# Block 2 of a two-block trunk: weights of four leading tiles split ahead of the stage before, norm sums on TensorE alone, transposed-weight dots in block 1 only

## The chip, the cores and the metric

One NeuronCore of a Trainium2 chip. The metric is the device time of one execution in microseconds, the median of several runs. The kernel before took 1892.75 us (three runs, 1886.89 to 1897.9).

## The reference

Two transformer trunks follow one another on 256 tokens of width 1024. The first (block 1) has two layers with modulation, pooled, gated and latent attention mixers, and an MLP; its first layer also carries 256 context tokens. The second (block 2) has two layers, and each of them is

```
mod = silu(c) @ w_ada[l] + b_ada[l]            # six vectors of 1024
h = rmsnorm(x, g_mix_pre) * (1 + scale_a) + shift_a
y = hybrid_mixer(h, w_in, ...) @ w_out         # three attentions
x = x + gate_a * rmsnorm(y, g_mix_post)
h = rmsnorm(x, g_ffn_pre) * (1 + scale_f) + shift_f
x = x + gate_f * rmsnorm((silu(h @ w_g) * (h @ w_u)) @ w_down, g_ffn_post)
```

with a hidden width of 2816. Everything is float32.

## The kernel before

**Products.** A float32 product is made of three products of rounded parts: high by high, high by low, low by high (lines 150 to 152, the helper `mm` at L131). Activations stand transposed, 128 features on the partitions, 256 tokens along the row. A weight piece is brought from HBM by SP's queue (`wraw`, 1 MB, two buffers), and `split` turns each half of it, a granule of 128 x 1024, into `whi` (a cast on ScalarE, L134) and `wlo` (a subtraction on VectorE, L135), with two buffers of each. A granule serves 24 matmuls. So a piece can be loaded two ahead and split one or two ahead of TensorE.

**Order.** The kernel is written as a recording in program order; a scheduler then fixes one list per engine, and each engine runs its list in order and waits by semaphores. What stands in a list ahead of a waiting instruction is done, what stands behind it is not.

**Hand-overs of block 2.** Between two big stages stands a chain: the last product gives `y`, the squares of `y` (`Post`) give `st`, from that come `ms` (VectorE), its power -0.5 (POOL), and a transposed copy `bc`; then for each of eight chunks k `update(k)` forms `post = y * G * bc` and `x = x + post`, and `Lead.chunk(k)` forms `xa = x * A` in a high part (ScalarE) and a low part (VectorE). TensorE doesn't wait for the next rmsnorm: it multiplies the unnormed `xa` by the first four tiles of the next weight matrix, chunk by chunk (`lead`), into the banks pa and pS, then two more tiles into pg and pmod (`tiles_x`). The norm's scale `rr` comes meanwhile (`norm_stats`) and is multiplied in when the tiles are read out (`lead_out`, which forms `lb`, `sgl`, `swu`). The following tiles get their granules by the common rings, and `h` is formed only then.

The function `first` (from L1035) does this for the weights w: `early` splits two tiles of w[0] into the rings, `early_act` splits two tiles of w[1] into eight small tiles `wact`, `early_more` two tiles of w[2] into `wmore0` and `wmore1`. All three are called at the start of `first`, so after the products of the stage before. w is w_in_2a of layer 0, w_gate_up of layer 0, w_in_2a of layer 1, and w_gate_up of layer 1. The stage ahead of a w_gate_up is w_out_2, whose input `mixc` has eight chunks: four are multiplied while the last mixers still run, the other four here, in four pieces (`gemm_half`; 24 products each, `x<-pa,x` at L1080 adds the parts).

**Sums of squares.** `norm_stats` squares the eight chunks on ScalarE (`sq`, L1109), POOL adds the first six (L1113), and TensorE sums over partitions by one-column products with ones (`pqt`): three pairs, one for the sum and two for the last chunks. In `update` the additions `x = x + post` (L1479) are on VectorE for k in ADDV = 1, 3, 5, 7 and on POOL for the others.

**Dots.** Part of the modulation vectors are products of a transposed weight row block with silu(c): 512 KB brought by SP (`wdot`, three buffers) and one VectorE instruction with a running sum (L436) for each 128 values; 128 such dots in all. They are queued as due, and every weight piece gives a credit of `self.pace`; a whole credit runs one dot. The pace is 3.25 in the MLP of block 1's layer 0, 0.75 in layer 1, 0.75 in the feed-forward of block 2 while any are due.

Of the kernel before, what the change touches and what calls it, by code (L numbers as in the profile page):

```python
# [21 lines left out]
S = 256  # L22
DFF = 2816
EPS = 1e-6
ADDV = 1, 3, 5, 7
PACE1 = 3.4
GAN = 1152
RAWN = 2080
# [2 lines left out]
class K:  # L31
# [994 lines left out]
    def block2(self):  # L1026
        tc, nc, a = self.tc, self.nc, self.a
        y = [x[:, 256:512] for x in self.x]
        with ExitStack() as es:
            act = es.enter_context(tc.tile_pool(name="bact", bufs=16, reuse_waits="tile"))  # L1030
            self.pump()
            self.pace = 0
            xs = [x[:, :256] for x in self.x]

            def first(stage, w, mods, f=None):  # L1035


                self.early(w[0], 2, 8)
                self.early_act(w[1], act)
                xp = stage.enter_context(tc.tile_pool(name="xin2", bufs=1, reuse_waits="tile"))  # L1040
                with tc.tile_pool(name="wmore", bufs=1, side="right", reuse_waits="tile") as wmp:
                    more = self.early_more(w[2], wmp)
                    lead = Lead(self, xp, mods)
                    if f:
                        f.rstd()
                    for k in range(8):
                        if f:
                            f.update(k)
                        lead.chunk(k)
                    o = self.lead(lead.xa, 4, by_k=f is not None)  # L1050
                    rr = xp.tile([128, 512], F32, name="rr")
                    out = self.norm_stats(rr[:, :256]) if f else self.first_stats(rr)
                    o = [p[0] for p in o]
                    for p in self.tiles_x(lead.xa[0], more=more, banks=(self.psum("pg"), self.pm.tile([128, 512], F32, name="pmod", tag="pmod"))):
                        o.append(p)
                        if len(o) == 5:
                            out()
# [9 lines left out]
            stage = ExitStack()  # L1067
            for l in range(2):
                m = lambda s: self.mod(1, l, s)[:, 0]
                if l == 0:  # L1070
                    A = self.gain(self.g_pre[:, l], m(1), "A10")
                    nc.vector.tensor_mul(A, A, self.g_final)
                    o = first(stage, a["w_in_2a"][0], [(0, 256, A, m(0))])
                with tc.tile_pool(name=f"bmix{l}", bufs=1, reuse_waits="tile") as mp:
                    mix = self.mixers2(l, *o, act, mp, y)
                    self.act_set("silu_and_others")
                    f = Post(self, y)

                    def ev(k, o):
                        nc.vector.tensor_add(y[k], o, y[k])  # L1080
                        f.chunk(k)
                    for i in range(4):
                        self.gemm_half(a["w_out_2"][l, i], mix, 0, 0, 256, lambda j, o, i=i: ev(2 * i + j, o))
                    del mix
                stage.close()
                f.gain(self.g_post[:, l], m(2))
                o = first(stage, a["w_gate_up"][l], [(0, 256, self.gain(self.f_pre[:, l], m(4), "A20"), m(3))], f)
                if self.due:
                    self.dots_begin(stage.enter_context(tc.tile_pool(name="dw2", bufs=1, reuse_waits="tile")))
                    self.pace = 0.75  # L1090
                with tc.tile_pool(name=f"bhid{l}", bufs=16, reuse_waits="tile") as hp:
                    f = self.ffn(l, *o, hp, y, act)
                self.dots_end()
                self.pace = 0
                stage.close()
                if l == 0:
                    f.gain(self.f_post[:, l], m(5))
# [343 lines left out]
class Post:  # L1441
# [193 lines left out]
```

## Time and profile before

| quantity | value |
|---|---|
| median of three runs | 1892.75 us |
| profiled execution | 1901.53 us, span 1899.8 us |
| mean granted clock of TensorE in it | 0.949 of full speed |
| TensorE busy | 1735.2 us (91%), 11998 matmuls |
| VectorE busy | 1243.1 us (65%) |
| ScalarE busy | 848.9 us (45%) |
| POOL busy | 242.9 us (13%) |
| HBM read | 297.72 MB, 157 GB/s over the span |

All durations below are of the profiled execution. Block 1 ends near 1160 us. The w_out_2 products of layer 0 end near 1311 us, its feed-forward near 1520 us, the w_out_2 products of layer 1 near 1677 us, its feed-forward near 1889 us. The granted clock is a share of 2.4 GHz; a stretch at 0.62 is a mixture of the two levels 2.4 and 1.2 GHz. Where a matmul's own time is shown, neighbours overlap in it; the distance from start to start tells what one costs.

### The profile page before, as it was taken

Reading aid. Unit: us, or ns where it says so; the run is one execution under the profiler, and the core shown is the slowest. Engines: PE = TensorE matmul, PEld = TensorE weight load, DVE = VectorE, ACT = ScalarE, POOL = GpSimd, SP = SyncE. Lnnn points to the kernel's source line nnn. Section 1 sums busy time; section 2 is a strip of 40 time slices with the busy share of each in tenths; the row PEclk is TensorE's granted clock in tenths of the full one; section 3 lists DMA queues with packets and bytes.
Section 4 is the critical chain, followed back from the end, with each engine's and each line's share of the span. In section 5 each row is a group of like instructions: output and inputs, shape, how many; then the busy total and the mean of one; then the engine's idle time right before and its main releaser. Section 6 shows DMA issues by size and latency. Waiting matters only on the chain.

```text
span 1899.8 us, 30418 instructions
## 1 busy us (share of the span) xinstructions
PE 1735.2 (91%) x11998; PEld 1484.0 (78%) x11998; DVE 1243.1 (65%) x2401; ACT 848.9 (45%) x1626; POOL 242.9 (13%) x264
## 2 busy tenths in 40 slices
PE   5998899989999999888989999797899989988997
PEld 3766546868777888874778999687899978788997
DVE  3237776588988846557778666657854665575555
ACT  3243434353222234544454446555444455554443
POOL 2025310110000001243110001202100031021000
PEclk9998989989999999997989999898999988989998
DMA  8533231287877622311278554216455523143553
GB/s 328 200 111 123 83 107 30 93 285 286 283 279 283 212 90 91 116 51 38 64 266 296 181 181 159 97 38 233 167 178 184 185 99 107 47 143 133 178 181 131
DMA packets 66639, 300.75 MB, mean 158 GB/s; under 512 B 9472, under 2 KB 13492, under 8 KB 45760
## 3 DMA queue, kind: packets, MB, share of 16 engines
q1 hardware_dynamic: 65744, 297.74, 45.0%
q8 instruction: 95, 1.56, 0.3%
q0 software_dynamic: 464, 1.05, 0.2%
q14 instruction: 48, 0.39, 0.1%
q10 hardware_dynamic: 288, 0.01, 0.0%
HBM read 297.72 MB, written 1.05 MB: 157 GB/s over the span
## 4 chain that ended last, share of the span: by engine, by line
PE 67%; DVE 12%; DMA 6%; ACT 3%; POOL 3%; issue 2%; ACTq 0%; SPq 0%; POOLq 0%; DVEq 0%
PE pa L131 48%; PE pS L131 6%; PE pb L131 3%; PE pg L131 3%; DVE wlo L135 3%; PE pO L131 3%; DMA wdot<-in_w_ada_t_dram 2%; DVE wdot L436 2%; DMA wdot<-in_w_mod_t_dram 1%; PE pmod L131 1%; PE pPT L942 1%; ACT whi L134 1%; DMA mraw<-in_w_mod_dram 1%; DVE Qz L815 1%; DVE nt L354 1%
## 5 line engine op out<-in xcount | busy, mean ns | idle before, releaser
L134 ACT CAST whi<-wraw 128x1024 fp32r<-128x1024 f32 (+4 forms) x398 | 371.1, 934 | 577.7 <-PE pa L131 519.8
L135 DVE TENSOR_TENSOR wlo<-wraw,whi 128x1024 fp32r<-128x1024 f32 (+4 forms) x398 | 434.5, 1094 | 232.0 <-ACT whi L134 231.2
L131 PE MATMUL pa<-h,whi 128*128 128x256 f32 (+1 forms) x2400 | 532.7, 318 | 9.9 <-ACT h L358 6.0
L131 PEld LDWEIGHTS pa<-h,whi 128*128 128x128 f32 x2400 | 399.0, 193 | 44.6 <-ACT h L358 7.4
L131 PE MATMUL pa<-h,wlo 128*128 128x256 f32 (+1 forms) x1200 | 381.5, 318 | 2.3 <-DVE wlo L135 2.1
L131 PE MATMUL pa<-hid,whi 128*128 128x256 f32 (+1 forms) x1728 | 378.0, 315 | 0.2
L131 PEld LDWEIGHTS pa<-hid,whi 128*128 128x128 f32 x1728 | 282.7, 188 | 23.6 <-issue 1.8
L131 PE MATMUL pa<-hid,wlo 128*128 128x256 f32 (+1 forms) x864 | 273.3, 316 | 8.7 <-DVE wlo L135 8.5
L131 PEld LDWEIGHTS pa<-h,wlo 128*128 128x128 f32 x1200 | 231.1, 193 | 20.6 <-DVE wlo L135 4.0
L131 PEld LDWEIGHTS pa<-hid,wlo 128*128 128x128 f32 x864 | 162.6, 188 | 22.7 <-DVE wlo L135 11.8
L436 DVE SCALAR_TENSOR_TENSOR wdot<-wdot,cb 128x1024 f32<-128x1024 f32 x128 | 155.9, 1228 | 25.2 <-DMA wdot<-in_w_ada_t_dram 14.5
L131 PE MATMUL pa<-mixc,whi 128*128 128x256 f32 (+1 forms) x512 | 121.5, 325 | 4.0 <-ACT whi L134 1.0
L131 PEld LDWEIGHTS pa<-mixc,whi 128*128 128x128 f32 x512 | 85.9, 194 | 16.9 <-issue 2.7
L131 PE MATMUL pa<-xa,whi 128*128 128x258 f32 x448 | 92.4, 300 | 6.4 <-ACT whi L134 4.5
L131 PE MATMUL pb<-whi,h 128*128 128x256 f32 (+2 forms) x448 | 93.4, 300 | 3.5 <-ACT h L358 3.3
L499 DVE SCALAR_TENSOR_TENSOR x<-pa,mod,x 128x256 f32<-128x256 f32 x144 | 63.0, 479 | 40.9 <-PE pa L131 40.3
L131 PEld LDWEIGHTS pb<-whi,h 128*128 128x128 f32 x448 | 74.1, 197 | 10.9 <-issue 6.1
L131 PE MATMUL pa<-mixc,wlo 128*128 128x256 f32 (+1 forms) x256 | 81.4, 320 | 1.0 <-DVE wlo L135 1.0
L131 PEld LDWEIGHTS pa<-xa,whi 128*128 128x128 f32 x448 | 76.5, 206 | 7.0 <-ACT whi L134 4.9
L329 POOL TENSOR_TENSOR sq<-sq 128x512 f32<-128x512 f32 (+1 forms) x15 | 18.9, 1260 | 427.8 <-ACT sq L325 427.8
L131 PE MATMUL pa<-xa,wlo 128*128 128x258 f32 x224 | 66.4, 299 | 3.5 <-DVE wlo L135 3.5
L131 PE MATMUL pb<-wlo,h 128*128 128x256 f32 (+2 forms) x224 | 65.9, 297 | 0.9 <-DVE wlo L135 0.9
(383 smaller groups left out, 2525.8 us busy)
## 6 DMA issues: line engine op xcount, KB each, us to landing
wdot<-in_w_ada_t_dram SPq DMA_DIRECT2D x96, 512.0 KB, 5.6
wraw<-in_w_gate_up_dram SPq DMA_DIRECT2D x44, 1024.0 KB, 4.9
wraw<-in_w_up_dram SPq DMA_DIRECT2D x32, 1024.0 KB, 4.9
wraw<-in_w_down_dram SPq DMA_DIRECT2D x32, 1024.0 KB, 5.7
mraw<-in_w_mod_dram SPq DMA_DIRECT2D x48, 512.0 KB, 4.2
wdot<-in_w_mod_t_dram SPq DMA_DIRECT2D x32, 512.0 KB, 5.4
wraw<-in_w_down_2a_dram SPq DMA_DIRECT2D x16, 1024.0 KB, 4.9
wraw<-in_w_in_2a_dram SPq DMA_DIRECT2D x12, 1024.0 KB, 4.8
```

The lines of the kernel that those rows point to most:

```text
L131: self.last = self.nc.tensor.matmul(out, l, r, start=start, stop=stop, **k).ins
L134: self.nc.scalar.copy(hi, src)
L135: self.nc.vector.tensor_sub(lo, src, hi)
L329: (eng or nc.vector).tensor_add(s, s, q)
L354: nc.vector.scalar_tensor_tensor(t[:, s], self.x[k][:, s], A[:, k:k + 1], bc[:, s], op0=ALU.mult, op1=ALU.mult)
L436: nc.vector.scalar_tensor_tensor(w, w, 1.0, c, op0=ALU.mult, op1=ALU.mult, accum_out=o[:, j:j + 1])
L499: nc.vector.scalar_tensor_tensor(self.x[n][:, s], o[:, s], gate()[:, r, n:n + 1], self.x[n][:, s], op0=ALU.mult, op1=ALU.add)
L815: nc.vector.tensor_mul(z[rows, :, r], e[rows], q[rows])
L942: nc.tensor.transpose(pt[:, n * 128:(n + 1) * 128], P[:, 0, n * 128:(n + 1) * 128], self.ident)
```

## The change

1. A new function `prepare(w)` opens the memory of the next hand-over and does the splits of w[1] (`wact`) and w[2] (`wmore`). It is called ahead of the w_out_2 products (both layers) and ahead of the last quarter of the down products (`down(2)` of layer 0). `first` then only splits w[0] and goes on. The raw piece of `wmore` gets a buffer of its own (`wmraw`).
2. `norm_stats` makes no POOL additions: all eight squares go to TensorE, 16 one-column products in place of 6, from one ring of two buffers.
3. `update` makes all its eight additions on VectorE (ADDV is gone).
4. The pace of the dots is 3.6 and 1.15 in block 1; block 2 runs none.

```diff
     def early_more(self, src, pool):
-        raw = self.raw_piece(src, 2048)
+        raw = pool.tile([128, 2048], F32, name="wmraw")
+        self.nc.sync.dma_start(raw, src)
...
-                self.pace = (3.25, 0.75)[l]
+                self.pace = (3.6, 1.15)[l]
...
+            def prepare(w):
+                stage.close()
+                xp = stage.enter_context(tc.tile_pool(name="xin2", bufs=1, side="right", reuse_waits="tile"))
+                wmp = ExitStack()
+                wm = wmp.enter_context(tc.tile_pool(name="wmore", bufs=1, side="right", reuse_waits="tile"))
+                self.early_act(w[1], act)
+                return w, xp, wmp, self.early_more(w[2], wm)
-            def first(stage, w, mods, f=None):
+            def first(prep, mods, f=None):
+                w, xp, wmp, more = prep
                 self.early(w[0], 2, 8)
-                self.early_act(w[1], act)
-                xp = stage.enter_context(tc.tile_pool(name="xin2", bufs=1, reuse_waits="tile"))
-                with tc.tile_pool(name="wmore", bufs=1, side="right", reuse_waits="tile") as wmp:
-                    more = self.early_more(w[2], wmp)
-                    lead = Lead(self, xp, mods)
+                lead = Lead(self, xp, mods)
...
-                    self.act_set("silu_and_others")
-                    f = Post(self, y)
+                self.act_set("silu_and_others")
+                prep = prepare(a["w_gate_up"][l])
+                f = Post(self, y)
...
-                o = first(stage, a["w_gate_up"][l], [(0, 256, self.gain(self.f_pre[:, l], m(4), "A20"), m(3))], f)
-                if self.due:
-                    self.dots_begin(stage.enter_context(tc.tile_pool(name="dw2", bufs=1, reuse_waits="tile")))
-                    self.pace = 0.75
+                o = first(prep, [(0, 256, self.gain(self.f_pre[:, l], m(4), "A20"), m(3))], f)
...
     def norm_stats(self, rr):
-        s = None
         for k in range(8):
-            q = self.tp.tile([128, 512], F32, name="sq", tag="sq" if k else "ssq", bufs=2)[:, :256]
+            q = self.tp.tile([128, 512], F32, name="sq", tag="sq", bufs=2)[:, :256]
             nc.scalar.activation(q, xs[k], AF.Square)
-            if k == 0:
-                s = q
-            elif k < 6:
-                nc.gpsimd.tensor_add(s, s, q)
-            if k >= 5:
-                for i in range(2):
-                    self.mm(st[:, i:i + 1], (s if k == 5 else q)[:, i * 128:(i + 1) * 128], self.ones[:, :1], k == 5 and i == 0, k == 7, skip_group_check=True)
+            for i in range(2):
+                self.mm(st[:, i:i + 1], q[:, i * 128:(i + 1) * 128], self.ones[:, :1], k == 0 and i == 0, k == 7, skip_group_check=True)
...
         if l == 0:
+            prep = prepare(a["w_in_2a"][1])
             f = Post(self, y)
         down(2)
...
-        (nc.vector if k in ADDV else nc.gpsimd).tensor_add(x, x, t)
+        nc.vector.tensor_add(x, x, t)
```

How the lists change is shown at three places of layer 1's hand-over (w_out_2 to w_gate_up). First ScalarE, from the last `mixc` (before). `whi_16468` belongs to w_out's third piece (the pieces 0 and 1, the latter `whi_16428`, stand ahead of it), `sq` are the squares of `y`.

```order
L134 CAST whi_16428<-wraw_16426 128x1024
L1403 ACTIVATE gsq_16234,gss_16235<-on_16173 128x256
L1414 ACTIVATE mixc_15199<-pot_16242,c_g_group_8211 128x128
L1414 ACTIVATE mixc_15200<-pot_16242,c_g_group_8211 128x128
L134 CAST whi_16468<-wraw_16466 128x1024
L1452 ACTIVATE sq_16407<-x_85 128x256
L1452 ACTIVATE sq_16423<-x_85 128x256
```

The same place now, where `whi_16434` is piece 0, `whi_16473` piece 1, `whi_16513` piece 2:

```order
L133 CAST whi_16434<-wraw_16432 128x1024
L1412 ACTIVATE mixc_15202<-pot_16245,c_g_group_8248 128x128
L1412 ACTIVATE mixc_15203<-pot_16245,c_g_group_8248 128x128
L1450 ACTIVATE sq_16452<-x_85 128x256
L133 CAST wmore0_16425<-wmraw_16423 128x1024
L133 CAST wmore1_16428<-wmraw_16423 128x1024
L1450 ACTIVATE sq_16468<-x_85 128x256
L133 CAST whi_16473<-wraw_16471 128x1024
L133 CAST whi_16513<-wraw_16511 128x1024
```

Ahead of the last `mixc` only piece 0 is split, and the casts of `wmore` and one square more stand ahead of piece 1. On VectorE the list from the same `mixc` was this, with `wlo_16429` of piece 1 four rows earlier:

```order
L135 TENSOR_TENSOR wlo_16429<-wraw_16426,whi_16428 128x1024
L295 TENSOR_SCALAR ms_16238<-gss_16235 128x1
L1406 TENSOR_SCALAR on_16173<-on_16173,grs_16237 128x256
L1415 SCALAR_TENSOR_TENSOR mixc_15199<-pot_16242,c_g_group_8211,mixc_15199 128x128
L1415 SCALAR_TENSOR_TENSOR mixc_15200<-pot_16242,c_g_group_8211,mixc_15200 128x128
L1080 TENSOR_TENSOR x_85<-pa_16393,x_85 128x256
L1080 TENSOR_TENSOR x_85<-pa_16409,x_85 128x256
L135 TENSOR_TENSOR wlo_16469<-wraw_16466,whi_16468 128x1024
```

And now it is this, with `wlo_16435` of piece 0 and `wlo_16474` of piece 1:

```order
L134 TENSOR_TENSOR wact_16414<-wraw_16397,wact_16414 128x256
L134 TENSOR_TENSOR wlo_16435<-wraw_16432,whi_16434 128x1024
L1413 SCALAR_TENSOR_TENSOR mixc_15202<-pot_16245,c_g_group_8248,mixc_15202 128x128
L1413 SCALAR_TENSOR_TENSOR mixc_15203<-pot_16245,c_g_group_8248,mixc_15203 128x128
L1089 TENSOR_TENSOR x_85<-pa_16438,x_85 128x256
L1089 TENSOR_TENSOR x_85<-pa_16454,x_85 128x256
L134 TENSOR_TENSOR wmore0_16425<-wmraw_16423,wmore0_16425 128x1024
L134 TENSOR_TENSOR wmore1_16428<-wmraw_16423,wmore1_16428 128x1024
L1454 TENSOR_TENSOR sq_16452<-sq_16452,sq_16468 128x256
L134 TENSOR_TENSOR wlo_16474<-wraw_16471,whi_16473 128x1024
```

The two `wmore` subtractions, which stood among the `xa` of the lead, and the eight `wact`, which stood ahead of `ms`, are here. On TensorE the end of the lead was followed by the three pairs of one-column products (`pqt`), by `pg`, and by the copy of the norm's scale (`c_ident,rs`):

```order
L131 MATMUL pa_16661<-xa0_16606,wlo_16563 128x258
L131 MATMUL pqt_16759<-ones_92,sq_16761 128x1 x2
L131 MATMUL pqt_16759<-ones_92,sq_16780 128x1 x2
L131 MATMUL pqt_16759<-ones_92,sq_16784 128x1 x2
L131 MATMUL pg_16791<-xa0_16606,wmore0_16600 128x258 x20
L1122 MATMUL pqt_16817<-c_ident_90,rs_16760 128x128 x2
```

Now there are eight pairs, the last four of them as follows:

```order
L130 MATMUL pqt_16762<-ones_92,sq_16780 128x1 x2
L130 MATMUL pg_16799<-xa0_16609,wmore0_16425 128x258 x2
L130 MATMUL pqt_16762<-ones_92,sq_16784 128x1 x2
L130 MATMUL pg_16799<-xa0_16609,wmore0_16425 128x258 x8
L130 MATMUL pmod_16800<-xa0_16609,wmore1_16428 128x258 x2
L130 MATMUL pqt_16762<-ones_92,sq_16788 128x1 x2
L130 MATMUL pmod_16800<-xa0_16609,wmore1_16428 128x258 x3
L130 MATMUL pqt_16762<-ones_92,sq_16792 128x1 x2
L130 MATMUL pmod_16800<-xa0_16609,wmore1_16428 128x258 x6
L1119 MATMUL pqt_16825<-c_ident_90,rs_16763 128x128 x2
```

The copy of the scale stands behind 31 of the `pg` and `pmod` products, where it stood behind 20. The lists also hold 105 dots in layer 0 of block 1 and 23 in layer 1, and none in block 2.

## Rows read from the trace of the kernel before

**Rows 1.** The page's chain that ended last, share of the span by engine.

```profile
PE 67%; DVE 12%; DMA 6%; ACT 3%; POOL 3%; issue 2%; ACTq 0%; SPq 0%; POOLq 0%; DVEq 0%
```

**Rows 2.** Stretches at T3: us from:to, length, busy (x) by engine, PEclk, DMA.

```profile
1662.00:1676.00 14.00, 13.14 (x92) 12.32 (x92) 8.84 (x18) 6.51 (x13) 0.00 (x0) 0.90 0.55 186
1676.00:1689.50 13.50, 6.38 (x31) 5.69 (x31) 11.14 (x22) 8.29 (x19) 4.95 (x6) 0.62 0.42 156
...
1709.00:1733.00 24.00, 17.69 (x119) 16.70 (x117) 14.57 (x28) 11.85 (x22) 5.00 (x4) 0.86 0.26 88
```

**Rows 3.** Stretches from the first post of T1 and T3 to the feed-forward's end.

```profile
1314.00:1520.30 206.30, 197.96 (x1608) 196.31 (x1608) 134.66 (x212) 95.96 (x154) 13.47 (x14) 0.97 0.54 185
1682.50:1889.00 206.50, 197.90 (x1607) 196.63 (x1607) 121.13 (x182) 95.69 (x153) 15.38 (x14) 0.97 0.45 153
```

**Rows 4.** Dots alone in two stretches; sum of all engines, 440 to 682 us.

```profile
400.00:690.00 290.00, 110.84 (x182) 1.00 0.72 257
...
1303.00:1358.00 55.00, 12.16 (x20) 0.88 0.61 214
...
sum 242.00, PE 235.89 PEld 188.51 DVE 204.46 ACT 70.51 POOL 0.00; mean PE 47.18 PEld 37.70 DVE 40.89 ACT 14.10 POOL 0.00
```

**Rows 5.** Lines by form, from 1150 us: xcount | busy us, mean ns | idle before.

```profile
L135 DVE TENSOR_TENSOR wlo<-wraw,whi 128x1024 fp32r<-128x1024 f32 x150 | 183.8, 1227 | 112.0 <-ACT whi L134 111.7
...
L134 ACT CAST whi<-wraw 128x1024 fp32r<-128x1024 f32 x150 | 156.8, 1047 | 193.1 <-PE pa L131 188.6 <-DMA wraw<-in_w_gate_up_dram 1.8 <-DMA wraw<-in_w_in_2a_dram 1.3
...
L1113 POOL TENSOR_TENSOR sq<-sq 128x256 f32<-128x256 f32 x15 | 13.1, 871 | 9.9 <-ACT sq L1109 5.6 <-issue 3.7
...
L1479 POOL TENSOR_TENSOR x<-x,post 128x256 f32<-128x256 f32 x12 | 11.3, 942 | 8.7 <-DVE post L1478 8.5
```

**Rows 6.** Timeline of VectorE at T3: start us, length us, instruction [idle before].

```profile
1664.89 0.76 DVE L1080 TENSOR_TENSOR x<-pa,x 128x256 f32<-128x256 f32 x2 [1.42 <-PE pa L131]
...
1678.08 2.77 DVE L135 TENSOR_TENSOR wact<-wraw,wact 128x256 fp32r<-128x256 f32 x8
1680.76 0.15 DVE L295 TENSOR_SCALAR ms<-st 128x2 f32<-128x2 f32 x1
1682.48 1.27 DVE L1478 SCALAR_TENSOR_TENSOR post<-x,pg,bc 128x256 f32<-128x256 f32 x3 [1.57 <-PE bc L1468]
...
1685.65 2.89 DVE L135 TENSOR_TENSOR wmore<-wraw,wmore 128x1024 fp32r<-128x1024 f32 x2
1688.46 1.83 DVE L1438 SCALAR_TENSOR_TENSOR xa<-x,A,xa 128x256 fp32r<-128x256 f32 x2
...
1690.55 0.47 DVE L1438 SCALAR_TENSOR_TENSOR xa<-x,A,xa 128x256 fp32r<-128x256 f32 x1
```

**Rows 7.** Timeline of ScalarE at T3, the first squares of y.

```profile
1666.05 0.72 ACT L1452 ACTIVATE sq<-x 128x256 f32<-128x256 f32 x2
```

**Rows 8.** Timeline of TensorE at T3.

```profile
1664.02 0.63 PE L131 MATMUL pa<-mixc,whi 128*128 128x256 f32 x2
...
1665.37 0.51 PE L131 MATMUL pa<-mixc,whi 128*128 128x256 f32 x2 [0.24 <-DVE x L1080]
...
1666.19 0.40 PE L131 MATMUL pa<-mixc,whi 128*128 128x256 f32 x2
...
1684.36 0.80 PE L131 MATMUL pS<-xa,wact 128*128 128x258 f32 x2 [1.92 <-ACT xa L1437]
...
1699.23 1.40 PE L131 MATMUL pqt<-ones,sq 128*128 128x1 f32 x12
...
1715.43 0.50 PE L131 MATMUL pa<-xa,whi 128*128 128x258 f32 x2 [3.74 <-ACT whi L134]
```

**Rows 9.** Timeline of VectorE at T3, after the lead.

```profile
1700.67 0.16 DVE L295 TENSOR_SCALAR ms<-pqt 128x2 f32<-128x2 f32 x1 [1.01 <-PE pqt L131]
...
1703.79 0.42 DVE L209 TENSOR_TENSOR sgl<-pa,rr 128x256 f32<-128x256 f32 x1 [0.46 <-ACT rr L1123]
```

**Rows 10.** Timeline of VectorE at T2.

```profile
1522.63 2.76 DVE L135 TENSOR_TENSOR wact<-wraw,wact 128x256 fp32r<-128x256 f32 x8
```

More of the change, by code (lines that the diff above doesn't have):

```diff
@@ L24 @@
 EPS = 1e-6
-ADDV = 1, 3, 5, 7
 PACE1 = 3.4
@@ L1033, in block2 @@
             xs = [x[:, :256] for x in self.x]
-            def first(stage, w, mods, f=None):
-                self.early(w[0], 2, 8)
-                self.early_act(w[1], act)
-                xp = stage.enter_context(tc.tile_pool(name="xin2", bufs=1, reuse_waits="tile"))
-                with tc.tile_pool(name="wmore", bufs=1, side="right", reuse_waits="tile") as wmp:
-                    more = self.early_more(w[2], wmp)
-                    lead = Lead(self, xp, mods)
-                    if f:
[L1045 to L1057, printed above, removed]
@@ new lines, in block2 @@
+            stage = ExitStack()
+            def prepare(w):
[7 more added lines that the diff above has]
+                w, xp, wmp, more = prep
+                self.early(w[0], 2, 8)
+                lead = Lead(self, xp, mods)
+                if f:
+                    f.rstd()
+                for k in range(8):
+                    if f:
+                        f.update(k)
+                    lead.chunk(k)
+                o = self.lead(lead.xa, 4, by_k=f is not None)
+                rr = xp.tile([128, 256 if f else 512], F32, name="rr")
+                out = self.norm_stats(rr[:, :256]) if f else self.first_stats(rr)
+                o = [p[0] for p in o]
+                for p in self.tiles_x(lead.xa[0], more=more, banks=(self.psum("pg"), self.pm.tile([128, 512], F32, name="pmod", tag="pmod"))):
+                    o.append(p)
+                    if len(o) == 5:
+                        out()
+                wmp.close()
@@ L1065, in first @@
                 return o, lead.xa[0], rr[:, :256], rest
-            stage = ExitStack()
             for l in range(2):
@@ L1072, in block2 @@
                     nc.vector.tensor_mul(A, A, self.g_final)
-                    o = first(stage, a["w_in_2a"][0], [(0, 256, A, m(0))])
+                    o = first(prepare(a["w_in_2a"][0]), [(0, 256, A, m(0))])
                 with tc.tile_pool(name=f"bmix{l}", bufs=1, reuse_waits="tile") as mp:
                     mix = self.mixers2(l, *o, act, mp, y)
-                    self.act_set("silu_and_others")
-                    f = Post(self, y)
-                    def ev(k, o):
-                        nc.vector.tensor_add(y[k], o, y[k])
-                        f.chunk(k)
@@ L1082, in block2, with ev @@
[L1082 to L1085, printed above, removed]
+                self.act_set("silu_and_others")
+                prep = prepare(a["w_gate_up"][l])
+                f = Post(self, y)
+                def ev(k, o):
+                    nc.vector.tensor_add(y[k], o, y[k])
+                    f.chunk(k)
+                for i in range(4):
+                    self.gemm_half(a["w_out_2"][l, i], mix, 0, 0, 256, lambda j, o, i=i: ev(2 * i + j, o))
@@ L1086, in block2 @@
+                del mix
                 f.gain(self.g_post[:, l], m(2))
-                o = first(stage, a["w_gate_up"][l], [(0, 256, self.gain(self.f_pre[:, l], m(4), "A20"), m(3))], f)
-                if self.due:
-                    self.dots_begin(stage.enter_context(tc.tile_pool(name="dw2", bufs=1, reuse_waits="tile")))
-                    self.pace = 0.75
+                o = first(prep, [(0, 256, self.gain(self.f_pre[:, l], m(4), "A20"), m(3))], f)
                 with tc.tile_pool(name=f"bhid{l}", bufs=16, reuse_waits="tile") as hp:
-                    f = self.ffn(l, *o, hp, y, act)
@@ L1093, in block2 @@
-                self.dots_end()
-                self.pace = 0
-                stage.close()
+                    f, prep = self.ffn(l, *o, hp, y, act, prepare)
                 if l == 0:
                     f.gain(self.f_post[:, l], m(5))
-                    o = first(stage, a["w_in_2a"][1], [(0, 256, self.gain(self.g_pre[:, 1], self.mod(1, 1, 1)[:, 0], "A10"), self.mod(1, 1, 0)[:, 0])], f)
+                    o = first(prep, [(0, 256, self.gain(self.g_pre[:, 1], self.mod(1, 1, 1)[:, 0], "A10"), self.mod(1, 1, 0)[:, 0])], f)
@@ L1099, in block2 @@
                 else:
                     self.post(y, self.f_post[:, l], m(5))
+            stage.close()
     def norm_stats(self, rr):
@@ L1168, in post, with ffn @@
             (nc.vector if k % 2 else nc.gpsimd).tensor_add(self.x[k][:, :256], self.x[k][:, :256], t)
-    def ffn(self, l, lead, xa, rr, rest, hp, y, act):
+    def ffn(self, l, lead, xa, rr, rest, hp, y, act, prepare):
         nc, a = self.nc, self.a
         self.ep = hp
-        f, h = None, []
+        f, prep, h = None, None, []
         groups = [range(0, 8), range(8, 16), range(16, 22)]
@@ L1234, in ffn @@
         if l == 0:
+            prep = prepare(a["w_in_2a"][1])
             f = Post(self, y)
         down(2)
-        return f
+        return f, prep
     def mixers2(self, l, lead, xa, rr, rest, act, mp, y):
```

## The prediction

> **What bounds the kernel now.** The chain of waits comes first: two thirds of the span end on TensorE [rows 1], so an edit pays or costs only where TensorE waits, or where its clock is low. The table by stretches shows where that is in the last layer: TensorE is nearly full while the second half of w_out is multiplied, then busy for 6.38 of 13.5 us at a granted clock of 0.62, and for 17.69 of 24 us further on [rows 2]. The same three stretches recur at each hand-over of block 2. I call them T1 (w_out to gate_up, layer 0), T2 (down to w_in, layer 1), T3 (w_out to gate_up, layer 1), and T0 for the entry from block 1. T3 is worked out in full, since the others carry the same instructions. In the timeline of T3 the reader follows three engines that each run their list in order: VectorE subtracts weights, then forms `ms`, waits for `bc`, runs `post` [rows 6]; ScalarE casts and squares [rows 7]; TensorE waits for either [rows 8].
>
> **1. The pace of the dots.** Block 2 loses its 11 dots, all in T1's feed-forward stage (x20 in the row counts each dot's read of the accumulator as well) [rows 4]. They were 11 times 1.23 us of VectorE, 13.5 us, but from the same point of T1 and of T3 the stages last 206.30 and 206.50 us, with 134.66 and 121.13 us of VectorE [rows 3]: with the dots and without them TensorE needs the same. Their removal is worth 0, by these two rows. The 11 go into layer 0 of block 1 (105 there instead of about 94). From 440 to 682 us of that stage TensorE is idle for 242.00 - 235.89 = 6.1 us while 110.84 us of dots and their reads run in the somewhat longer stage [rows 4]. If that idle time is the dots' own, a dot costs below 0.1 us, and 11 cost +1. The ends are 0 (all slack) and +6, should half of each 1.23 us be paid. I take +1, the nearest row.
>
> **2. Splits ahead of the w_out products (T1 and T3).** The 8 `wact` and 2 `wmore` splits leave the stretch after the last product. Removed there: `wact` stands between the last product and `ms`, 2.77 us with 2.68 to the next start (1678.08 to 1680.76) [rows 6], so -2.7.
>
> What they now displace: in the order of ScalarE the squares of the first two tiles and both 1024-wide casts stand ahead of `whi` of w_out's piece 1, and VectorE has `wmore0`, `wmore1` and an addition ahead of its `wlo`. Before, piece 1 was split ahead of the last `mixc`, and TensorE passed from piece 0 to piece 1 with a wait of 0.24 us at 1665.37 [rows 8]. Now, from the first `x` (done near 1665.3 [rows 6]): square 0.36 (half of 0.72 [rows 7]), two casts of 1.05 [rows 5], square 0.36, `whi` 1.05, to 1669.2. VectorE can subtract `wmore1` only after its cast, 1668.0 to 1669.2, then the addition 0.42 and `wlo` 1.23 [rows 5], to 1670.85. Piece 1 needs `wlo` for its third product, which ran at 1665.7: 5.1 us later. The other pieces follow on one another as before. Behind this wait TensorE starts at the lower clock: a pair of products takes 0.63 us where it takes 0.40 at the higher [rows 8], 0.115 each; 12 products as after the last wait give +1.4. Sum of the part: -2.7 + 5.1 + 1.4 = +3.8 at T3, and as much at T1. The ends are -2.7 (the wait covered) and +5.3 (24 products at the low clock, two squares late at the end).
>
> The `wact` splits themselves fall among the last mixer's steps, where both engines wait for TensorE and for each other; I give 0 for it. If this cover is missing, they delay `mixc` by at most their 2.7 us. The 2 MB asked for in that stretch pass the w_out pieces on SP's queue; TensorE then waits for an earlier split, not for SP, so 0.
>
> **3. The lead without wmore (T1, T2, T3).** `wmore` took 2.89 us of VectorE in the middle of the lead [rows 6]. The lead ran from 1684.36 to 1699.23, 14.9 us [rows 8]; its 96 products at 0.12 need 11.5. Of the 3.4 us the low clock at its start keeps about half. I take -1.7 at each; ends 0 and -2.9.
>
> **4. The norm by 16 one-column products.** Before, five POOL additions led to three pairs at the end of the lead. `ms` came 1.3 us after the lead, and the first `sgl` 3.1 us later [rows 9]. Now TensorE's order has all eight pairs behind the lead, with 25 of the `pg` and `pmod` products between them, since ScalarE has six squares behind its last `xa` and only two buffers for them. 25 products at 0.12 and 16 one-column products at 0.10 (12 took about 1.2 from start to the next [rows 8, 9]) give 4.7 us, so `ms` is 3.4 us later, and `rr`, `sgl` and the list behind them with it. At T3 TensorE then waits 3.74 us for ScalarE's `whi` at 1715.43 [rows 8], which stands behind that list: the lateness is paid. +3.4 at each of T1, T2, T3; ends 0 (the list has slack) and +4.5 (the squares' round trips).
>
> **5. T2 and T0.** At T2 `wact` lies between `ms` and `post`, 2.76 us [rows 10], where the chain over `bc` alone takes 1.72 (1680.76 to 1682.48 [rows 6]): -1.0. With parts 3 and 4: -1.0 - 1.7 + 3.4 = +0.7. Its `wmore` is split inside the feed-forward, where VectorE has 71 to 85 us to spare [rows 3]. T0 has no row of its own kind after the change (the lead's input lies in other memory and starts later, the squares start sooner); I give 0, with ends of -3 and +4, the size of part 4 either way.
>
> **6. POOL's additions to VectorE.** 12 additions of x move, four at a place, of 0.94 us on POOL [rows 5] and 0.42 on VectorE [rows 6]: 1.7 us of VectorE at a place, under a lead of 14.9 us; 0 while the lead hides it. A pair of `xa` took 1.83 us at 1688.46, just when POOL was adding, where one alone takes 0.47 [rows 6]: 0.9 us lost. Relief of one such pair per place is -0.9, and lies within part 3's ends.
> The Trainium skill, "SBUF — State Buffer", says that a VectorE instruction with two SBUF inputs and a GpSimd instruction exclude one another for their whole length. The trace bears it out in direction (0.9 us for each of the slowed `xa`, 0.47 alone); by the rule alone the change would gain what POOL's additions hold up, which is the second rival.
>
> **Sum.** Parts 2, 3, 4: +3.8 - 1.7 + 3.4 = +5.5 at T1 and at T3, 11.0. T2 +0.7, T0 0, dots +1: **+12.7 us**. On the profiled execution (1901.53 us, span 1899.8) that is 1914; it lies 8.8 us above the median of the three runs, 1892.75, so a median of about **1906**. What a measurement of this kernel can tell from no change is about 0.5%, 9.5 us: 1883.3 and 1902.2 are the bounds.
>
> **The rivals.**
> - *The clock stays up (faster).* For it: T3 pays for a low clock twice, 0.62 in 13.5 us and 0.86 in 24 us [rows 2]. If the shorter wait behind w_out keeps TensorE at the higher level, about 20 products at 0.115 (2.3 us) and 0.28 of 24 us at half speed (3.4 us) come back, 5.7 at each of three places, and the 1.4 of part 2 twice: 12.7 - 17.1 - 2.8 = -7.2, and with the lead at its full -2.9 (1.2 more at three places) -10.8: 1882. Against it: the wait behind w_out shrinks by a third only, and a new one opens after piece 0. It decides where the granted clock of the stretch from the last w_out product to the lead's first products is above 0.9. The Trainium skill, "TensorE: Matmul & The Clock Gate", has an idle TensorE lose its clock as well; the trace agrees with its 0.62.
> - *Traded one for one (no change).* The lock of part 6: at each place 5 additions of 0.87 and 4 of 0.94 us leave POOL [rows 5], 8.1 us, against 1.7 us more on VectorE. If a third of the net 6.4 us was VectorE's own waiting, it is -2.1 at three places, and +12.7 becomes +6.4: 1899. For it: the slowed `xa`. Against: POOL was busy for 15.38 of 206.50 us [rows 3], and its additions lie mostly beside ScalarE's work.
> - *The dots were not free (slower still).* If the 11 more in block 1 pay 0.55 us each (+6), and the splits hold up `mixc` at T1 and T3 (+2.7 each): 12.7 + 5 + 5.4 = +23: 1916. For it: that stage moves 0.72 of the DMA share [rows 4].
> - *The change doesn't do what it says.* Excluded by the orders: the splits, the 16 products and the missing dots are there.
>
> **How the numbers follow.** Forecast 1906 with 0.54 (its own range 1898 to 1914, of which about a seventh lies under 1902.2), clock 0.13 with a spread of 1876 to 1888, trade 0.23 with 1893 to 1903, slower still 0.10. Slower by over 0.5%: 0.46 + 0.10 = 0.56; within: 0.08 of the forecast, 0.21 of the trade, 0.03 of the clock, together 0.30 (rounded down from 0.32); faster: 0.14. The range, 1882 to 1922, cuts the lower half of the clock's case and the top of the last.
>
> **What would show it.** Right: after piece 0 of w_out at T1 and T3 a wait of TensorE of 4 to 6 us that ends on `wlo` or `whi`; the first `post` 1 to 5 us later behind the first `x` than now (1664.89 to 1682.48, 17.6 us [rows 6]); `ms` of the norm 4 to 5.5 us behind the lead instead of 1.3; the 3.74 us wait grown to about 7; T1's feed-forward no shorter. Wrong: no wait after piece 0, or a first `sgl` as soon after the lead as now, or block 1 longer by more than 3 us, or a clock above 0.9 where 0.62 stood.

## The result, and the profile after

The changed kernel took 1916.05 us against 1893.02 (ratio 1.0138, 95% interval 1.0096 to 1.018), and when it was timed again with more runs 1912.88 against 1895.56 (1.0085, 1.005 to 1.0121): slower, by about 17 to 23 us where 13 were forecast.

Executions of one kernel differ by 2%, with TensorE's mean granted clock (from 0.959 to 0.942 the kernel before goes from 1878 to about 1903 us). So a second measure is given below: **at equal clock** is the mean distance of a kernel's runs from a straight line of time over mean clock, drawn through the runs of the kernel before that were timed beside it, with twice its standard error; runs in a slower state of the chip are left out. It takes out what an edit does by the mean clock as well. For the changed kernel it is +15.1 ± 2.1 us.

The page after: less POOL, the same VectorE, 0.5 MB less read, and again two thirds of the chain on TensorE (answers to [rows 1]).

```profile
PE 1748.9 (92%) x12058; PEld 1499.4 (79%) x12058; DVE 1241.2 (65%) x2413; ACT 846.8 (44%) x1625; POOL 216.6 (11%) x237
...
PE 67%; DVE 12%; DMA 6%; ACT 4%; POOL 2%; issue 2%; ACTq 0%; SPq 0%; DVEq 0%; POOLq 0%
```

T3 cut at the same events (the first of the last two `mixc`, called the last `mixc` from here on, last w_out product, first lead product, last lead product, last product on `xa`), first before, then after; columns as in [rows 2].

```profile
1661.90:1675.90 14.00, 13.10 (x92) 12.32 (x92) 8.81 (x17) 6.48 (x13) 0.00 (x0) 0.90 0.56 187
1675.90:1684.40 8.50, 1.37 (x8) 0.85 (x7) 6.06 (x16) 4.36 (x12) 2.00 (x3) 0.65 0.61 222
1684.40:1699.40 15.00, 14.94 (x107) 14.74 (x107) 10.39 (x19) 8.06 (x18) 7.40 (x8) 0.86 0.23 86
1699.40:1725.20 25.80, 20.82 (x151) 20.40 (x152) 19.02 (x43) 13.68 (x28) 6.68 (x5) 0.87 0.25 82
```

```profile
1664.50:1685.40 20.90, 17.19 (x97) 16.04 (x96) 12.43 (x20) 9.07 (x15) 0.00 (x0) 0.72 0.64 223
1685.40:1691.60 6.20, 2.12 (x16) 1.70 (x15) 4.70 (x11) 2.31 (x5) 0.70 (x1) 0.85 0.43 143
1691.60:1705.80 14.20, 14.20 (x101) 14.20 (x101) 7.51 (x21) 4.22 (x10) 0.00 (x0) 0.82 0.04 18
1705.80:1734.30 28.50, 23.06 (x179) 22.43 (x178) 19.40 (x43) 15.72 (x34) 3.69 (x5) 0.88 0.22 75
```

The second half of w_out is 6.9 us longer, at a clock of 0.72 for 0.90. The hand-over is 2.3 us shorter, the lead 0.8. What follows the lead is 2.7 us longer.

**w_out.** TensorE's timeline after (answers to [rows 8]):

```profile
1665.89 0.58 PE L130 MATMUL pa<-mixc,wlo 128*128 128x256 f32 x1 [0.27 <-DVE wlo L134]
...
1669.75 0.28 PE L130 MATMUL pa<-mixc,wlo 128*128 128x256 f32 x1
1673.02 1.22 PE L130 MATMUL pa<-mixc,whi 128*128 128x256 f32 x4 [2.99 <-ACT whi L133]
1674.69 0.58 PE L130 MATMUL pa<-mixc,wlo 128*128 128x256 f32 x1 [0.45 <-DVE wlo L134]
```

And ScalarE, then VectorE, in the same place (answers to [rows 6, 7]):

```profile
1669.31 0.42 ACT L1450 ACTIVATE sq<-x 128x256 f32<-128x256 f32 x1 [2.81 <-DVE x L1089]
1669.72 1.99 ACT L133 CAST wmore<-wmraw 128x1024 fp32r<-128x1024 f32 x2
1671.62 0.41 ACT L1450 ACTIVATE sq<-x 128x256 f32<-128x256 f32 x1
1671.94 1.03 ACT L133 CAST whi<-wraw 128x1024 fp32r<-128x1024 f32 x1
```

```profile
1670.07 0.42 DVE L1089 TENSOR_TENSOR x<-pa,x 128x256 f32<-128x256 f32 x1 [0.79 <-PE pa L130]
1670.80 2.36 DVE L134 TENSOR_TENSOR wmore<-wmraw,wmore 128x1024 fp32r<-128x1024 f32 x2 [0.31 <-ACT wmore L133]
1673.08 0.42 DVE L1454 TENSOR_TENSOR sq<-sq 128x256 f32<-128x256 f32 x1
1673.42 2.56 DVE L134 TENSOR_TENSOR wlo<-wraw,whi 128x1024 fp32r<-128x1024 f32 x2
```

This is the forecast wait, in the forecast order: square, two casts, square, `whi`. But it is 3.4 us (2.99 and 0.45), not 5.1, because TensorE reaches it later: 24 products of piece 0 stand behind the last `mixc`, where before 12 of them ran earlier, in waits of the mixers, since piece 0 too was split in time. All but the last few go at the low clock (pairs of 0.63 us), and so do 24 products behind the wait.

The order of the casts is not the whole reason. SP's queue in the same place, before, then after; the last two rows give SP's longest wait ahead of these requests, and the size of the request of 1664.98 with the time from issue to landing:

```profile
1648.05 12.60 SPq L242 DMA_DIRECT2D wraw<-in_w_out_dram  x4
```

```profile
1653.48 0.54 SPq L242 DMA_DIRECT2D wraw<-in_w_out_dram  x1
1664.53 0.33 SPq L229 DMA_DIRECT2D wmraw<-in_w_gate_up_dram  x1
1664.98 10.23 SPq L242 DMA_DIRECT2D wraw<-in_w_out_dram  x3
...
SPq L229 <- DVE on L1404: 9.7, 1, 9.7
...
wraw<-in_w_out_dram SPq DMA_DIRECT2D x1, 512.0 KB, 6.0
```

Before, all four pieces of w_out were asked for by 1660.65. Now `wmraw` stands behind piece 0 in SP's list, and its request waits 9.7 us for VectorE's `on` of the last mixer. Piece 1 stands behind it, is asked for at 1664.98 and lands 6.0 us later, at 1671.0. The ring would have held it nearly as long: the last subtraction of `wact`, which frees its buffer, ends at 1664.70. `whi` starts at 1671.94, 0.9 us behind the landing. With no square and no cast ahead of it TensorE, done with piece 0 at 1670.03, would by an estimate from these rows still have waited 2.0 of the 2.99 us (landing at 1671.0, cast of 1.03).

**The norm.** TensorE and VectorE after the lead (answers to [rows 8, 9]):

```profile
1705.65 0.95 PE L130 MATMUL pqt<-ones,sq 128*128 128x1 f32 x8
...
1712.12 0.50 PE L130 MATMUL pqt<-ones,sq 128*128 128x1 f32 x4
...
1723.11 0.51 PE L130 MATMUL pa<-xa,whi 128*128 128x258 f32 x2 [1.62 <-ACT whi L133]
1727.24 0.58 PE L130 MATMUL pa<-xa,wlo 128*128 128x258 f32 x1 [3.62 <-DVE wlo L134]
```

```profile
1712.66 0.16 DVE L295 TENSOR_SCALAR ms<-pqt 128x2 f32<-128x2 f32 x1 [1.27 <-PE pqt L130]
...
1714.53 0.42 DVE L208 TENSOR_TENSOR sgl<-pa,rr 128x256 f32<-128x256 f32 x1 [1.65 <-ACT rr L1120]
```

Each one-column product is two matmuls, so the eight pairs are 32 matmuls where the three pairs were 12. The last pair stands 6.5 us behind the first. `ms` follows the first pair by 7.0 us where it followed by 1.4 (1699.23 to 1700.67), `sgl` by 8.9 us; before it was 4.6 (1699.23 to 1703.79).

Before, TensorE waited 3.74 us for `whi` here [rows 8] and then for `wlo`:

```profile
1717.17 0.58 PE L131 MATMUL pa<-xa,wlo 128*128 128x258 f32 x1 [1.24 <-DVE wlo L135]
```

That is 5.0 us in all, and now 5.2 (1.62 and 3.62). The wait didn't grow, since TensorE reaches it 3.4 us later behind the first pair: 20 more one-column matmuls and six more of `pg` and `pmod` stand ahead of it. But the wait ends 3.65 us later behind the first pair (1717.17 less 1699.23, 1727.24 less 1705.65), and that is the lateness that is paid.

**Feed-forward of layer 0.** It is 4.6 us longer, from the last product on `xa` to the last of down (162.3 before, 167.0 after). ScalarE there, after:

```profile
1500.11 2.56 ACT L133 CAST wact<-wraw 128x256 fp32r<-128x256 f32 x8 [0.28 <-DMA wraw<-in_w_in_2a_dram]
1505.30 1.56 ACT L133 CAST whi<-wraw 128x768 fp32r<-128x768 f32 x2 [2.63 <-DMA wraw<-in_w_down_2b_dram]
```

`wact`'s raw piece took one of the two ring buffers, so the next piece of down was asked for a piece late. TensorE waited 1.56 and 0.23 us for its `whi`.

### The profile page after: what moved, and what is told of

It is laid out like the page before. It is cut to its first block, busy times and chain, and to the rows that moved or that the text cites. A ratio compares the mean times of both kernels' runs of the same rounds, so it can differ in the third digit from the quotient of the medians.

```text
span 1909.4 us, 30536 instructions
## 1 busy us (share of the span) xinstructions
PE 1748.9 (92%) x12058; PEld 1499.4 (79%) x12058; DVE 1241.2 (65%) x2413; ACT 846.8 (44%) x1625; POOL 216.6 (11%) x237
## 3 DMA queue, kind: packets, MB, share of 16 engines
q8 instruction: 95, 1.56, 0.3%
## 4 chain that ended last, share of the span: by engine, by line
PE 67%; DVE 12%; DMA 6%; ACT 4%; POOL 2%; issue 2%; ACTq 0%; SPq 0%; DVEq 0%; POOLq 0%
PE pa L130 47%; PE pS L130 6%; PE pg L130 3%; DMA wdot<-in_w_ada_t_dram 3%; PE pb L130 3%; DVE wlo L134 3%; PE pO L130 3%; DVE wdot L436 2%; ACT whi L133 2%; PE pPT L942 1%; PE pmod L130 1%; DVE nt L354 1%; DVE Qz L815 1%; POOL rs L296 1%; PE pqt L130 1%
## 5 line engine op out<-in xcount | busy, mean ns | idle before, releaser
L436 DVE SCALAR_TENSOR_TENSOR wdot<-wdot,cb 128x1024 f32<-128x1024 f32 x128 | 156.3, 1233 | 21.8 <-DMA wdot<-in_w_ada_t_dram 13.6
L130 PE MATMUL pa<-mixc,whi 128*128 128x256 f32 (+1 forms) x512 | 126.5, 336 | 8.4 <-ACT whi L133 6.9
L130 PEld LDWEIGHTS pa<-mixc,whi 128*128 128x128 f32 x512 | 91.2, 206 | 20.8 <-ACT whi L133 8.3
```

The costliest lines, as they stand in the source:

```text
L130: self.last = self.nc.tensor.matmul(out, l, r, start=start, stop=stop, **k).ins
L436: nc.vector.scalar_tensor_tensor(w, w, 1.0, c, op0=ALU.mult, op1=ALU.mult, accum_out=o[:, j:j + 1])
```

## The experiments

The table gives the lengths in us, from start to start, between the same events in each kernel's own profile: w = last `mixc` to last w_out product, h = last product to first lead product, l = first lead product to last product on `xa`. The sum is that of all eight, as a difference from before.

| kernel | T1 w, h, l | T2 h, l | T3 w, h, l | sum | ratio (95%) | at equal clock |
|---|---|---|---|---|---|---|
| before | 13.4, 8.2, 39.8 | 7.1, 37.3 | 13.7, 8.7, 40.6 | 168.8 | 1 | 0 |
| changed | 20.5, 6.0, 42.7 | 5.8, 38.7 | 20.6, 6.4, 42.5 | +14.4 | 1.0138 (1.0096-1.018) | |
| e12 the same | 20.9, 6.0, 42.1 | 5.8, 38.5 | 20.5, 6.0, 42.7 | +13.7 | 1.0085 (1.005-1.0121) | +15.1 ± 2.1 |
| e1 norm only | | | | | 1.0082 (1.0042-1.0123) | +8.8 ± 3.4 |
| e2 old norm | 20.7, 6.0, 38.7 | 5.8, 35.7 | 20.5, 6.0, 38.8 | +3.4 | 1.0103 (1.0058-1.0148) | +7.9 ± 2.4 |
| e3 late | 13.2, 9.6, 42.3 | 5.3, 38.4 | 13.3, 9.6, 42.7 | +5.6 | 1.008 (1.004-1.0121) | +12.2 ± 2.4 |
| e4 late, old norm | 13.2, 9.6, 36.8 | 5.2, 36.5 | 12.9, 9.6, 35.4 | -9.6 | 0.999 (0.9955-1.0025) | -1.6 ± 2.8 |
| e11 the same | 13.3, 9.6, 36.9 | 5.2, 36.4 | 14.1, 9.6, 34.6 | -9.1 | 0.9979 (0.9941-1.0017) | -2.1 ± 1.8 |
| e5 dots only | | | | | 1.0001 (0.9966-1.0036) | +1.4 ± 2.7 |
| e6 wmore early | 15.5, 7.6, 38.6 | 7.0, 34.8 | 15.6, 7.6, 39.3 | -2.8 | 1.0053 (1.0017-1.0089) | +9.3 ± 1.9 |
| e7 T2 late | 20.9, 6.0, 42.1 | 5.5, 38.1 | 20.5, 6.0, 42.9 | +13.2 | 1.007 (1.004-1.0101) | +12.5 ± 1.5 |
| e8 late, 5 buffers | 13.0, 9.6, 38.9 | 5.5, 41.0 | 13.2, 9.6, 39.1 | +1.1 | 1.0043 (1.0009-1.0078) | +9.7 ± 2.2 |
| e9 additions only | 13.5, 8.7, 38.6 | 7.2, 37.9 | 14.1, 10.0, 41.3 | +2.5 | 0.9975 (0.9938-1.0012) | +0.4 ± 2.7 |
| e10 rstd first | 13.3, 7.4, 38.5 | 5.7, 37.7 | 13.1, 7.4, 38.2 | -7.5 | 1.0041 (1.001-1.0072) | +1.4 ± 2.6 |

Where a row has no lengths, the profile has a much lower clock than the others.

**e1**: the kernel before with the new `norm_stats` alone (the edit of the change's part 2).

> The kernel before with the 16 one-column products in norm_stats alone. Theory (the last pairs stand behind the lead and pg, so rr is 3.4 us late at each of three places and the list behind it is on the path): ms 4 to 5.5 us behind the lead in place of 1.3, about +10 us, 1903. Rival (the lists have slack; the slowdown is all from the early splits): 1893, same.

+8.8 ± 3.4 at equal clock. The rival falls; the norm alone makes the kernel slower.

**e2**: the changed kernel with the old `norm_stats`.

> The changed kernel with the old norm_stats (POOL adds, three pairs). Theory: the norm's part goes, the wait behind piece 0 of w_out stays at about 3 us at T1 and T3: 1916 - 10 = 1906. Rival (all of it is the splits): 1916. Rival (the norm is all of it): 1895.

l is 4.0, 3.0 and 3.7 us shorter than in the changed kernel, 10.7 in all (10 expected), and w stays at 20.5. At equal clock both rivals fall: each half costs about 8 us, and 8.8 + 7.9 is near the whole. The ratios don't tell as much: those of e1, e2 and e12 lie within one another's intervals.

**e3**: the changed kernel with `prepare` behind the products.

```diff
-                prep = prepare(a["w_gate_up"][l])
...
-                o = first(prep, [(0, 256, self.gain(self.f_pre[:, l], ...
+                o = first(prepare(a["w_gate_up"][l]), [(0, 256, self.gain(self.f_pre[:, l], ...
```

(and the same for w_in_2a of layer 1.)

> The changed kernel with prepare called after the w_out and down products in the program (the scheduler may still move the splits among the last pieces), 16-product norm kept. Theory: no wait behind piece 0 of w_out, no wait for a late down piece at layer 0; the norm's lateness stays: 1893 + 10 less 5 for leads without wmore, 1898. Rival (not the place of the splits but the memory, the dots or POOL's missing additions cost): near 1916.

The wait behind piece 0 is gone and w is 13.2 again. Two rows of TensorE's timeline at T3, the second the only later wait of w_out:

```profile
1668.97 0.78 PE L130 MATMUL pa<-mixc,whi 128*128 128x256 f32 x3 [0.46 <-ACT mixc L1410]
...
1678.57 0.47 PE L130 MATMUL pa<-mixc,whi 128*128 128x256 f32 x2 [0.22 <-DVE x L1088]
```

But h is 9.6. The splits moved, they did not vanish: on VectorE they now stand between the last product and `ms`.

```profile
1682.49 2.09 DVE L134 TENSOR_TENSOR wact<-wraw,wact 128x256 fp32r<-128x256 f32 x6
1684.50 1.23 DVE L134 TENSOR_TENSOR wmore<-wmraw,wmore 128x1024 fp32r<-128x1024 f32 x1
1685.64 2.36 DVE L134 TENSOR_TENSOR wlo<-wraw,whi 128x1024 fp32r<-128x1024 f32 x2
1687.91 0.16 DVE L295 TENSOR_SCALAR ms<-st 128x2 f32<-128x2 f32 x1
```

The expected 1898 was missed: 1908.8, with 1891.5 for the kernel before beside it. At equal clock it is 2.9 us better than the changed kernel, less than the nearly 8 of w + h over both places; the two intervals leave about 0 to 6.

**e4** and **e11**: e3 with the old `norm_stats`, timed twice.

> The changed kernel with prepare after the products and the old norm_stats: both suspected costs away, what is left is wmore's own raw buffer, eight additions on VectorE, the dots' pace. Theory: leads 1.7 us shorter at three places and no new cost: 1886, faster than before. Rival (a third cost in what is left): 1900 or more.

> The version with the splits after the products and the old norm_stats once more, beside the others of this call. Its stages add up to about 9 us less than before in the profile: 1884. Rival (its first timing, 0.999, is the whole truth): 1891.

The stages are 9 us shorter than before, the time 2 us (at equal clock; both ratios' intervals hold 1). No third cost of the size of the two is left, but a gain isn't shown either. A part of what the stages promise is lost beside the eight stretches: in e11's profile T0 is 2.5 us longer than before and the two feed-forwards 0.6 and 2.2, in e4's 0.8, 0.6 and 0.8. In e3's they are 2.3, 2.3 and 0.7 us longer, and with them its +5.6 becomes +10.9, near its +12.2. What is left over in e4 and e11 stays open.

**e5**: the kernel before with the new pace of the dots, none in block 2.

> The kernel before with the new pace of the dots alone (3.6 and 1.15 in block 1, none in block 2). Theory (TensorE doesn't need the VectorE time that T1's 11 dots take, and layer 0 of block 1 has slack): within 2 us of before, 1892. Rival (the dots cost more where DMA is busiest): layer 0's MLP 6 us longer, 1898. Rival (T1 gains 13 us of VectorE): 1885.

No difference that shows: 1.0001, and +1.4 ± 2.7. VectorE's 13.5 us at T1 were spare, and block 1 took the 11 dots in at no cost that shows.

**e6**: e2 with `early_act` called in `first`; only `early_more` stays in `prepare`.

> The changed kernel with the old norm_stats, where prepare splits wmore alone ahead of the products and wact is split in first, after them. Theory (wact's raw piece takes one of the two ring buffers ahead of w_out's piece 1, and that pushes piece 1 behind the splits; wmore's has a buffer of its own): no wait behind piece 0, w_out's second half 13.4 us from the last mixc as before in place of 20.5, 13 us less than the 1903.7 of the version with both early: about 1890. Rival (any split called ahead of the products does it): 1904.

w falls from 20.5 to 15.5: five of the seven us go with the early `wact`. Its raw piece leaves the ring, and SP now asks for all four pieces of w_out ahead of `wmraw`, as at T3:

```profile
1659.62 12.59 SPq L242 DMA_DIRECT2D wraw<-in_w_out_dram  x4
1673.31 0.33 SPq L229 DMA_DIRECT2D wmraw<-in_w_gate_up_dram  x1
```

The edit moves both at once, so what the ring does and what SP's order does is not separated. With only `wmore` early, pieces 0 and 1 are split in time again. The two us that are left are `wmore` itself, now ahead of an `x` that a later piece's bank waits for:

```profile
1295.37 0.97 PE L130 MATMUL pa<-mixc,whi 128*128 128x256 f32 x3 [0.46 <-ACT mixc L1418]
1307.20 0.47 PE L130 MATMUL pa<-mixc,whi 128*128 128x256 f32 x2 [2.48 <-DVE x L1089]
```

The time stays near e2's (+9.3 against +7.9 at equal clock), though the sum fell by 6: the expected 1890 was missed (1901.9). T0 and the feed-forwards are 3.2, 2.4 and 0.8 us longer than before, but e2's are 0.8, 5.0 and 1.4, so why is open.

**e7**: the changed kernel with `prepare` for w_in_2a of layer 1 called behind the down products.

> The changed kernel with prepare for w_in (T2) called after the down products, all else as changed. Theory: the wait of 1.8 us for a late down piece goes, the hand-over from the last down product to the lead is up to 1.3 us longer again: 2 us less, 1914; visible in the feed-forward's length (166.9 to about 164.5) rather than in the median. Rival (the longer feed-forward comes from T1's late list alone): the 1.8 us wait goes but the length stays 166.9.

The wait of 1.8 us is gone, and the feed-forward is 164.6 us long, as expected to 0.1 us. In the time, the 2.6 us to e12 (12.5 for 15.1) are about what the two intervals leave open.

**e8**: e3 with five buffers for the norm's squares.

```diff
-            q = self.tp.tile([128, 512], F32, name="sq", tag="sq", bufs=2)[:, :256]
+            q = pool.tile([128, 256], F32, name="sq", tag="sqn", bufs=5)
```

> The version with prepare after the products and 16 products in the norm (1908.8), with five buffers for the norm's squares in place of two. Theory (two buffers hold six squares back behind the lead): ms from 7.6 to about 5 us behind the lead, rr from 9.1 to about 6.5, 2.6 us less at each of three places: about 1901. Rival (the pairs stand behind the lead in TensorE's list whatever the buffers): 1909, rr at 9.1.

Ten of the 16 products now stand right behind the lead, and `ms` comes 2 us sooner at T1 and T3 (5.6 for 7.6 us behind the lead's last product in pS). l is 3.4 and 3.6 us shorter there. T2 is 2.6 us longer, and the time by 2.5 us less, within the two intervals: in the stages the buffers are part of the norm's cost, in the time it isn't shown.

**e9**: the kernel before with `ADDV = tuple(range(8))`.

> The kernel before with all eight additions of x in update on VectorE, nothing else. Theory (1.7 us more VectorE at each of three places, hidden by the lead, and POOL out of VectorE's way): 0 to -3 us, 1890. Rival (VectorE is the bound of the lead): +1.7 at three places, 1898.

+0.4 ± 2.7: moving four additions per place to VectorE costs nothing that shows.

**e10**: e4 with `f.rstd()` called ahead of the splits and `early_more` behind the second chunk.

> The version with the splits after the products and the old norm_stats (1888.7), with rstd ahead of the splits in the program and wmore called behind the second chunk: ms stands ahead of half of wact, of wmore1 and of both wlo on VectorE. Theory (these splits between the last product and post are what makes the hand-over of that version 9.6 us in place of 8.2 and 8.7): 2 us less at T1 and T3, 1885, faster than before by about 0.4%. Rival (the lead waits for the splits anyway): 1889.

h falls by 2.2 us at both places, as expected, but l grows by 1.6 and 3.6 against e11: the splits taken from the hand-over are missing behind it. No gain: the expected 1885 was missed, at 1899.2 with 1893.3 for the kernel before.

**e12**: the changed kernel again.

> The changed kernel itself once more, with as many runs as the experiments have. Theory (the norm's part and the splits' part add up, with nothing else in the change): at equal mean clock 8.8 + 7.9 = 17 us above before, a ratio near 1.010. Rival (parts overlap or a further cost is in the combination): under 12 or over 22 us at equal clock.

15.1 ± 2.1, near the 16.7 of the two halves.

The halves don't simply add up in every version. At equal clock the new norm costs 8.8 us on the kernel before (e1) and 7.2 with the early splits (e12 less e2), but 13.8 with the late ones (e3 less e4). The early place of the splits costs 9.5 with the old norm (e2 less e4), but 2.9 with the new one (e12 less e3). Why late splits and the new norm together are dearer than the sum is open.

## Why the prediction came out as it did

The sign, the places and the two main steps were right; +12.7 stands against +15.1 ± 2.1 at equal clock, and against +14 in the stages of T1 to T3 and 7.7 outside them in the first profile (feed-forwards 4.6 and 0.7, T0 2.4). That the sum came so near is in part luck: parts 2 and 4 each hold errors that offset one another, and part 5 missed a cost.

Of the signs named, two came as they were told: the first `post` starts 20.9 us behind the first `x` for 17.6 (1668.85 to 1689.78), and T1's feed-forward is no shorter. Three came otherwise: the wait behind piece 0 is 3.4 us for 4 to 6, `ms` comes 6.9 us behind the lead for 4 to 5.5, and the wait of 3.74 us did not grow to 7.

1. *Dots, +1.* e5: +1.4 ± 2.7, which holds 1 as well as 0. The upper end, half of each 1.23 us, is 6.8 and not 6.
2. *Splits ahead of w_out, +3.8 a place.* w and h together: +4.9 and +4.6. The terms were off on both sides: the wait was 3.4 us in place of 5.1, but 12 products of piece 0 came behind the last `mixc` as well, which the working did not have, and 24 products behind the wait went at the low clock, where 12 were reckoned. The order shown in the change had the first: piece 0's `wlo` right ahead of `mixc`. The saving of 2.7 ahead of `ms` came as 2.2 and 2.3. The step that failed is that TensorE waits for an earlier split and not for SP, so 0: piece 1 was asked for at 1664.98 behind `wmraw`, landed at 1671.0, and that alone makes some 2 us of the wait. The casts ahead of `whi`, from which the wait was reckoned, end only 0.9 us later.
3. *Lead without wmore, -1.7.* From the first lead product to the last one in pS 14.5, 14.3, 14.3 us became 13.8, 13.7, 13.5: -0.7, not -1.7. Too large: the start at the low clock stayed (0.86 before, 0.82 after).
4. *Norm, +3.4 a place.* l of the changed kernel less l of e2: 4.0, 3.0, 3.7. The size is right and it is paid, as e1 shows without the splits, but the working is not. It took 16 products at 0.10 us from a row in which 12 matmuls are six products, so there were 32, and 28 of `pg` and `pmod` between them, not 25: at T3 `ms` is 5.6 us later behind the first pair, not 3.4. `sgl` is only 4.3 us later, since POOL's power takes less time (below), and the end of the wait on `wlo` 3.65. That the late list is what is paid, and not the added products alone, e8 supports: with the same products and `ms` 2 us sooner, l is 3.4 and 3.6 us shorter at T1 and T3.
5. *T2 +0.7, T0 0.* T2: +0.1, with the hand-over 1.3 us shorter (1.0 forecast). T0: +2.4 in the first profile, +0.8 in e12 (39.4 for 38.6 us); the lead of T0 ran at 0.89 in the first and at 1.00 in the second. The step that failed here is the sentence that the splits inside the feed-forward cost nothing since VectorE has 71 to 85 us to spare: spare time of an engine says nothing about the ring. It cost 2.3 us (e7). Of the other 2.3 us, 1.5 are a wait of 0.99 us for `sgl` and one of 0.47 for `wlo`, some 7 us into the products on `h`. They are new in layer 0, where e2, e3, e6, e7, e8, e10 and also e5, with only the dots gone, have them, but not e4 and e11; in layer 1 every kernel has them, that before too. So they are not a cost of the splits alone, and their cause is open.
6. *Additions on VectorE, 0.* Nothing that shows (e9: +0.4 ± 2.7).

The rival of the clock fell: in the stretch that was to decide, from the last w_out product to the lead, the clock rose from 0.65 to 0.85, below the 0.9 it asked for, and with the new wait w_out itself ran at 0.72 in place of 0.90. The rival of the dots had 1916, which is what the first timing gave, but not by its mechanism: e5 shows no price of the dots, and the last mixers are not held up (from T2's last product on `xa` to the last `mixc` 97.5 us before, 94.9 after). The trade was not seen in the time (e9). That VectorE and POOL stand in each other's way is seen once more, in POOL's power behind `ms`, before (with two `wlo` beside it on VectorE) and after (alone):

```profile
1700.90 1.69 POOL L296 TENSOR_TENSOR rs<-ms,mhalf 128x2 f32<-128x2 f32 x1 [5.26 <-DVE lb L208]
```

```profile
1712.90 0.70 POOL L296 TENSOR_TENSOR rs<-ms,mhalf 128x2 f32<-128x2 f32 x1 [23.64 <-DVE lb L207]
```

In the block 2 part of all fourteen profiles this power takes 0.69 to 0.71 us where no `wlo` is running as it starts, and 1.61 to 1.69 where one is. It agrees with the Trainium skill, "SBUF — State Buffer", section "SBUF: two separate sides", by which VectorE, in an instruction with two SBUF inputs, and GpSimd hold the ports that they share one at a time, for a whole instruction. So `sgl` came 1.9 us behind `ms` in place of 3.1, and a part of the norm's lateness was paid back.

## What to carry to other kernels

A split that is done earlier takes its buffer earlier: count the ring's buffers of the stage that it is moved into, not the spare time of its engines. A buffer of its own doesn't settle it: if its request has to wait, as `wmraw`'s did for 9.7 us, every request behind it in the DMA queue's list waits as well. Work moved off the end of one stage lands in front of something in the next in-order list; look up what now stands behind it, and who waits for that. A reduction that feeds a chain is worth an idle engine's additions when the alternative queues behind TensorE's big products.

## What the runs showed that was not expected

The mixers of block 2, whose instructions are the same in all kernels, take about 95 to 102 us in most profiles and 109 to 115 in some, with the clock. Layer 0's, in e4 and e11, the same kernel twice (columns as in [rows 2]):

```profile
1190.90:1306.00 115.10, 103.58 (x617) 87.56 (x615) 57.79 (x154) 56.73 (x165) 13.23 (x18) 0.79 0.20 64
```

```profile
1184.90:1287.10 102.20, 89.95 (x616) 77.02 (x614) 57.80 (x154) 56.68 (x165) 12.79 (x18) 0.92 0.22 72
```

VectorE and ScalarE did the same work in both to 0.05 us; TensorE was busy 13.6 us longer. This is nearly as much as the whole change, and it is why stages were compared, not single executions. Before and after show it too: up to the first lead the unchanged code took 360.7 us at 0.93 and 348.3 at 0.96.

```profile
0.00:360.70 360.70, 316.23 (x2218) 214.48 (x2219) 200.25 (x449) 140.00 (x283) 81.86 (x89) 0.93 0.39 137
```

```profile
0.00:348.30 348.30, 305.04 (x2219) 208.66 (x2220) 199.53 (x449) 140.00 (x283) 82.43 (x89) 0.96 0.40 142
```
